# A transformer block on one core: the beginning reordered, and the q, k, v projection in five channel groups

## The chip, the core and the metric

One core of a Trainium2 chip runs the whole kernel as one program. The time is device microseconds of one execution; lower is better. TensorE multiplies matrices, VectorE (DVE) and ScalarE (ACT) work element by element, GpSimd (POOL) does almost nothing here, SyncE (SP) issues nearly all DMA transfers. Weights lie in HBM, working tiles in SBUF, and matmuls write to PSUM.

## The reference

One decoder layer on 256 tokens of width 2048, in float32:

```
mod = silu(c) @ w_ada + b_ada              # shift1, scale1, gate1, shift2, scale2, gate2
h   = rms_norm(x, norm1_gain) * (1 + scale1) + shift1
proj = h @ w_in                            # q, k, v of two attentions, q, k, v, r, a of a
                                           # gated linear attention, three branch gates
o_sb, o_dil, o_gla = the three token mixers on their columns
y   = g0 * (o_sb @ w_br_sb) + g1 * (o_dil @ w_br_dil) + g2 * (o_gla @ w_br_gla)
x   = x + gate1 * (y @ w_out)
h   = rms_norm(x, norm2_gain) * (1 + scale2) + shift2
x   = x + gate2 * ((silu(gate) * up) @ w_ffn_out)      # gate, up = split(h @ w_ffn_in)
```

All weights together are some 390 MB, and each is read once.

## The kernel before

**Matmuls in three parts.** Each float32 operand is split into a high part (`whi`, a cast to fp32r on ScalarE, line 142) and a low part (`wlo`, the difference, on VectorE, line 143). `mm3` (lines 147 to 150) multiplies high by high, high by low and low by high into one PSUM bank. `load_weights` (line 120) brings two chunks of 128 rows and 512 columns per DMA (512 KB) into `raw`, of which there are four buffers, as of `whi` and `wlo`. `block` (line 152) runs over the chunks of one block of 512 output columns and both tiles of 128 tokens. A block of all 16 chunks has 96 matmuls. There are four PSUM banks `acc` for these sums and four named `misc` for all else.

**The beginning** (lines 169 to 218, 324 to 351, 402 to 421). `crow`, `rows` and `brow` are small tiles into which c, the norm gains and the bias rows are loaded, to be transposed on TensorE into columns (`vec`, `bada`). They share the pool tag `scr` (three buffers) with the scratch tiles of all later work. `norm1` loads x in four pieces of 512 KB, squares it on ScalarE for the mean square (line 339), takes the inverse root per token tile (`rsqrt`, a chain of small operations on VectorE and ScalarE), scales x by it on ScalarE (line 346), transposes it in 32 transposes (line 350) and copies it from PSUM to `xT` (line 351).

**Shift and scale of norm 1** come from 2048 x 4096 of w_ada, for the channel chunks of one group at a time (`ada_group`, line 248). For each of 16 row chunks a tile with the shift and scale columns of the group is loaded (line 262) and multiplied by silu(c) and added on VectorE (`ada_mac`, lines 240 and 242). Then one column sum per chunk and segment on TensorE (`column_sum`, line 285) and small operations (lines 291 and 294) give two columns. `make_h` (line 355) applies them to `xT` and splits the result into the high and low h of that chunk (lines 360 to 362).

**Channel groups.** The 13 blocks of q, k, v columns are computed group by group over the 16 channel chunks, `GROUPS = ((0, 3), (3, 7), (7, 11), (11, 16))`, so that the first matmul needs shift and scale of three chunks only. While a group is multiplied, w_ada tiles of the next one are loaded and added, spread over the blocks (lines 423 to 433). After each group a block's sums leave PSUM: the first time as a ScalarE copy into an SBUF tile `A` (line 390), later as a VectorE addition onto it (line 392). The block with which a group ends is the one with which the next begins, and its sums stay in PSUM (`carried`): one block per boundary. The last group is mixed with the attentions (lines 699 to 705): blocks 0 to 4, stick-breaking attention, the gate columns of the linear attention (line 523, with its sum in an `acc` bank), blocks 9 to 12, the linear attention, blocks 5 to 8, the dilated attention. Behind them come the r and gate blocks, over all 16 chunks each.

**Order.** The program is written in order; a scheduler gives each engine a fixed order at build time, by priority. Loads and splits of weights, the w_ada work and the evacuations are given the priority of work 4000 instructions earlier (`prio`, line 97). `XAT = 4` says how many w_ada tiles of the first group are asked for before x. Each engine, SP among them, then goes through its own list in order, and one waiting instruction holds up what is behind it.

Of the kernel before, what the change touches and what calls it, by code (L numbers as in the profile page):

```python
# [17 lines left out]
P = 128  # L18
T = 256
# [14 lines left out]
XAT = 4  # L34
AHEAD = 4000
FIN = 13
GROUPS = ((0, 3), (3, 7), (7, 11), (11, 16))
# [27 lines left out]
def trunk(ctx: ExitStack, tc: tile.TileContext, I, out):  # L65
# [30 lines left out]
    @contextmanager  # L96
    def prio(offset=AHEAD):
        """Priority of work emitted ``offset`` instructions earlier; the count goes on."""
        with tc.high_priority(offset=offset):
            start = tc.cur_priority  # L100
            yield
            n = tc.cur_priority - start
        tc.cur_priority += n
# [15 lines left out]
    # ---------------------------------------------------------------- weights  # L119
    def load_weights(src, k0, k1, c0, w=NB, spare=()):  # L120
        """hi and lo parts of the 128-row chunks [k0, k1) of columns [c0, c0 + w).

        The last chunks go into the slots named in ``spare``, two slots for two chunks.
        """
# [27 lines left out]
    def block(pss, act, src, k0, k1, c0, base=0, w=None, tiles=range(NT), go_on=False, more=False):  # L152
        """pss[t] = act[:, chunks]^T @ src[chunks, c0:c0+512]; act(k, t) gives the hi and lo chunk."""
# [14 lines left out]
    # ---------------------------------------------------------------- constants  # L168
# [13 lines left out]
    crow = scr([P, P])  # L182
# [11 lines left out]
    rows = scr([P, P])  # L194
    brow = scr([P, P])
# [24 lines left out]
    def rsqrt(ss, inv_n, shape):  # L220
        """(ss * inv_n + EPS) ** -0.5, with a Newton step after the tables."""
# [12 lines left out]
    # ---------------------------------------------------------------- adaLN  # L234
# [13 lines left out]
    def ada_group(k0, k1, tags=ADA_TAGS, between=None):  # L248
        """shift and scale of norm 1 for the channel chunks [k0, k1): (scale + 1) * gain and shift as columns."""
# [37 lines left out]
    def finish_columns(ps, dst, seg, k0, gain_row=None):  # L287
        """adds the bias; with a gain, (scale + 1) * gain."""
# [9 lines left out]
    def ada_segment_steps(acc, seg):  # L298
        """multiply-adds of one segment; each runs well behind the load of its tile"""
# [21 lines left out]
    # ---------------------------------------------------------------- norm 1 and its transpose  # L321
    xT = [S(f"T{j}", [P, 4, T]) for j in range(4)]

    def norm1():
        xin = [S(f"A{9 + j}", [P, 2, NB]) for j in range(4)]
        for t in range(NT):
            for hf in range(2):
                nc.sync.dma_start(
                    xin[2 * t + hf].rearrange("p a b -> p (a b)"),
                    I["x"][t * P : (t + 1) * P, hf * 2 * NB : (hf + 1) * 2 * NB],  # L330
                )
        for t in range(NT):
            ss2 = small([P, 2])
            for hf in range(2):
                junk = scr([P, 512])
                xs = xin[2 * t + hf]
                pa = small([P, 2])
                for q in range(2):
                    nc.scalar.activation(junk, xs[:, q, :], AF.Square, accum_out=pa[:, q : q + 1])
                nc.vector.tensor_add(ss2[:, hf : hf + 1], pa[:, 0:1], pa[:, 1:2])  # L340
            ss = small([P, 1])
            nc.vector.tensor_add(ss, ss2[:, 0:1], ss2[:, 1:2])
            rstd = rsqrt(ss, 1.0 / D, [P, 1])
            for hf in range(2):
                xs = xin[2 * t + hf]
                nc.scalar.activation(xs, xs, AF.Copy, scale=rstd)
                for q in range(2):
                    ps = misc_bank([P, 4, P])
                    for i in range(4):
                        nc.tensor.transpose(ps[:, i, :], xs[:, q, i * P : (i + 1) * P], ident)  # L350
                    nc.scalar.copy(xT[2 * hf + q][:, :, t * P : (t + 1) * P], ps)
# [3 lines left out]
    def make_h(k, sh, sc):  # L355
        """hi and lo of x * sc + sh for channel chunk k."""
# [11 lines left out]
    # ---------------------------------------------------------------- input projection (q, k, v), by channel groups  # L368
    w_in = I["w_in"]
    A = [None] * 13  # L370
    # one group ends with the block that the next begins with: its sums stay in PSUM
    up, down = list(range(13)), list(range(12, -1, -1))
    orders = (up[1:] + up[:1], up, down)
    carried = []

    def proj_block(g, b, w=None, carry=False):
        k0, k1 = GROUPS[g]
        go_on = bool(carried)
        pss = carried.pop() if go_on else [acc_bank() for _ in range(NT)]
# [43 lines left out]
    for g in range(len(GROUPS) - 1):  # L423
# [3 lines left out]
        for n, b in enumerate(orders[g]):  # L427
            while done < steps * (n + 1) // FIN and next(nxt, "end") != "end":
                done += 1
            proj_block(g, b, early if (g, n) == (0, 0) else None, carry=n == 12)  # L430
# [5 lines left out]
    # small constants, needed from here on  # L436
# [19 lines left out]
    def qk_norm(b, h0, h1, gain):  # L456
        """rms norm of the heads h0..h1 of block b, transposed in place to [channel, token]; gain(h) is a column."""
# [21 lines left out]
    # ---------------------------------------------------------------- stick-breaking attention  # L479
# [41 lines left out]
    # ---------------------------------------------------------------- gated linear attention  # L521
    def gla():
        aw = load_weights(w_in, 0, KC, COL_A, P)
        ps = acc_bank([P, T])
# [27 lines left out]
        # q and k by channel: [channel, head, token], in place  # L552
# [80 lines left out]
    # ---------------------------------------------------------------- dilated attention  # L633
    def dilated():
# [25 lines left out]
        # mixture of the groups: softmax over their log-denominators  # L660
# [19 lines left out]
        for j in range(2):  # L680
            o = misc_bank([P, T])
            for g in range(3):
# [5 lines left out]
                # transposed as [s, t]: (s0, t0) | (s0, t1) | (s1, t1)  # L688
# [18 lines left out]
    # ada segments in the background: gate1 as rows, shift2 and scale2 as columns  # L707
# [45 lines left out]
    # ---------------------------------------------------------------- r, branch gates  # L753
# [29 lines left out]
    # GLA output: norm gain and silu(r), transposed  # L783
# [253 lines left out]
```

## Time and profile before

| | us |
|---|---|
| median of three runs (1648.91 to 1657.99) | 1654.28 |
| span of the profiled execution, first to last instruction | 1657.5 |
| highest of the three runs | 1657.99 |
| TensorE busy with matmuls | 1608.4 |
| VectorE busy | 1158.9 |
| ScalarE busy | 777.5 |

The times do not say which run the profile is of; its span lies 0.5 us under the highest. In the lines of the profile, "out<-in" names the tiles written and read, "xN" counts instructions, and what stands in brackets is the idle time of the engine ahead of the instruction and what ended it. A line of the timeline gives start, time to the last end, engine, line and operation. A line of the windows view gives a stretch, its length, the busy time and number of instructions of each engine (PE, PE's weight loads, DVE, ACT, POOL), the granted clock of TensorE, the DMA share and GB/s. PE stands for TensorE.

### The profile page before, as it was taken

What the parts mean: (1) busy time and instruction counts of PE and PEld (TensorE: products, weight loads), DVE (VectorE), ACT (ScalarE), POOL (GpSimd) and SP (SyncE); (2) the same over time, 40 slices, a digit from 0 to 9 for tenths busy, and PEclk for the clock granted to TensorE, in tenths of its full rate; (3) what the DMA queues carried; (4) which work ended last, traced back from release to release, by engine and by line L of the source; (5) the groups of instructions that cost most, each with busy time, mean ns of one, the idle gap of its engine ahead of it and who ended that gap; (6) DMA issues with size and microseconds to landing.
All of it is one profiled execution on the core that took longest, in us unless ns stands there. A gap on an engine that the chain in (4) does not pass through costs nothing.

```text
span 1657.5 us, 20010 instructions
## 1 busy us (share of the span) xinstructions
PE 1608.4 (97%) x7293; PEld 1323.2 (80%) x7293; DVE 1158.9 (70%) x1399; ACT 777.5 (47%) x1075; POOL 5.9 (0%) x14
## 2 busy tenths in 40 slices
PE   4999999999999999999999999999999999999998
PEld 3778888788888878788777788788888888888887
DVE  6789997888997577758876578765555555555554
ACT  5654446556765433343435643453344443344442
POOL 1000000000000000000000000000000000000000
PEclk9999999999999999999999999999999999999999
DMA  9999986445797789879987488955666665666664
GB/s 312 319 318 320 329 288 203 140 141 189 255 309 251 234 272 317 281 253 315 304 277 250 137 304 308 310 180 191 194 190 189 194 188 189 193 197 187 188 202 135
DMA packets 194563, 395.93 MB, mean 239 GB/s; under 512 B 12898, under 2 KB 27912, under 8 KB 194464
## 3 DMA queue, kind: packets, MB, share of 16 engines
q1 hardware_dynamic: 194240, 394.63, 73.5%
q8 instruction: 57, 0.93, 0.2%
q14 instruction: 42, 0.34, 0.1%
q0 software_dynamic: 224, 0.01, 0.0%
HBM read 392.50 MB, written 2.10 MB: 238 GB/s over the span
## 4 chain that ended last, share of the span: by engine, by line
PE 83%; DMA 7%; DVE 5%; ACT 2%; issue 2%; SPq 0%; DVEq 0%; ACTq 0%
PE acc L149 26%; PE acc L150 26%; PE acc L148 26%; DMA araw<-w_ada 4%; DVE wlo L143 2%; DVE ada L242 1%; ACT whi L142 1%; DMA raw<-w_ffn_in 1%; PE misc L582 1%; PE misc L834 1%; PE misc L285 1%; DMA raw<-w_in 1%; DVE T L242 1%; DMA A<-x 0%; PE misc L476 0%
## 5 line engine op out<-in xcount | busy, mean ns | idle before, releaser
L143 DVE TENSOR_TENSOR wlo<-raw,whi 128x1024 fp32r<-128x1024 f32 (+1 forms) x547 | 652.1, 1197 | 381.5 <-ACT whi L142 379.3
L142 ACT CAST whi<-raw 128x1024 fp32r<-128x1024 f32 (+1 forms) x547 | 563.1, 1032 | 732.5 <-PE acc L150 562.3
L149 PE MATMUL acc<-wlo,H 128*128 128x512 f32 x1552 | 607.8, 392 | 3.4 <-DVE wlo L143 3.2
L148 PE MATMUL acc<-whi,H 128*128 128x512 f32 x1552 | 606.3, 392 | 2.2 <-ACT whi L142 2.1
L150 PE MATMUL acc<-whi,H 128*128 128x512 f32 x1552 | 607.5, 392 | 0.0
L149 PEld LDWEIGHTS acc<-wlo,H 128*128 128x128 f32 x1552 | 292.0, 188 | 65.8 <-DVE wlo L143 6.3
L148 PEld LDWEIGHTS acc<-whi,H 128*128 128x128 f32 x1552 | 291.9, 188 | 64.1 <-ACT whi L142 3.9
L150 PEld LDWEIGHTS acc<-whi,H 128*128 128x128 f32 x1552 | 292.0, 188 | 61.0 <-DVE H L362 0.9
L148 PE MATMUL acc<-whi,A 128*128 128x512 f32 x360 | 141.7, 394 | 2.7 <-ACT whi L142 2.7
L149 PE MATMUL acc<-wlo,A 128*128 128x512 f32 x360 | 141.8, 394 | 0.5 <-DVE wlo L143 0.5
L150 PE MATMUL acc<-whi,A 128*128 128x512 f32 x328 | 128.9, 393 | 0.0
L242 DVE SCALAR_TENSOR_TENSOR T<-araw,csil,T 128x1024 f32<-128x1024 f32 x60 | 76.2, 1281 | 17.1 <-DMA araw<-w_ada 16.9
L242 DVE SCALAR_TENSOR_TENSOR ada<-araw,csil,ada 128x1024 f32<-128x1024 f32 x60 | 76.2, 1280 | 13.6 <-DMA araw<-w_ada 13.4
L148 PEld LDWEIGHTS acc<-whi,A 128*128 128x128 f32 x360 | 68.3, 190 | 17.4 <-ACT whi L142 3.1
L149 PEld LDWEIGHTS acc<-wlo,A 128*128 128x128 f32 x360 | 68.2, 190 | 15.6 <-DVE wlo L143 1.4
L150 PEld LDWEIGHTS acc<-whi,A 128*128 128x128 f32 x328 | 62.3, 190 | 12.8
L392 DVE TENSOR_TENSOR A<-A,acc 128x512 f32<-128x512 f32 x72 | 48.0, 684 | 10.1 <-PE acc L150 9.8
L150 PE MATMUL acc<-whi,T 128*128 128x512 f32 x120 | 47.3, 394 | 0.0
L148 PE MATMUL acc<-whi,T 128*128 128x512 f32 x120 | 47.3, 394 | 0.0
L149 PE MATMUL acc<-wlo,T 128*128 128x512 f32 x120 | 47.2, 393 | 0.0
L242 DVE SCALAR_TENSOR_TENSOR ada<-OS,csil,ada 128x1024 f32<-128x1024 f32 (+2 forms) x33 | 35.5, 1075 | 0.8 <-DMA OS<-w_ada 0.6
L148 PE MATMUL acc<-whi,OS 128*128 128x512 f32 x80 | 32.0, 399 | 0.0
(292 smaller groups left out, 1129.2 us busy)
## 6 DMA issues: line engine op xcount, KB each, us to landing
raw<-w_in SPq DMA_DIRECT2D x205, 512.0 KB, 4.7
raw<-w_ffn_in SPq DMA_DIRECT2D x176, 512.0 KB, 3.9
araw<-w_ada SPq DMA_DIRECT2D x128, 512.0 KB, 5.0
raw<-w_ffn_out SPq DMA_DIRECT2D x88, 512.0 KB, 4.5
raw<-w_out SPq DMA_DIRECT2D x32, 512.0 KB, 5.5
OS<-w_ada SPq DMA_DIRECT2D x16, 512.0 KB, 9.4
raw<-w_br_gla SPq DMA_DIRECT2D x16, 512.0 KB, 5.9
raw<-w_in SPq DMA_DIRECT2D x26, 256.0 KB, 4.9
```

The source lines that it names most:

```text
L142: nc.scalar.copy(hi[:, :n, :], raw[:, :n, :])
L143: state["split"] = nc.vector.tensor_tensor(lo[:, :n, :], raw[:, :n, :], hi[:, :n, :].bitcast(F32), op=ALU.subtract)
L148: nc.tensor.matmul(ps, lh, rh, start=start, stop=False)
L149: nc.tensor.matmul(ps, lh, rl, start=False, stop=False)
L150: state["mm"] = nc.tensor.matmul(ps, ll, rh, start=False, stop=stop)
L242: nc.vector.scalar_tensor_tensor(acc, raw, c, acc, op0=ALU.mult, op1=ALU.add)
L285: nc.tensor.matmul(ps, acc, ones[:, 0:1], start=True, stop=True)
L392: nc.vector.tensor_add(A[b][:, t, :], A[b][:, t, :], pss[t])
L582: nc.tensor.matmul(ps[:, h, :], at(lhs, h, t), at(rhs, h, t), start=True, stop=True)
L834: nc.tensor.transpose(ps[:, i, :], src[:, i * P : (i + 1) * P], ident)
```

## The change

- `crow`, `rows` and `brow` get slots of their own (`H7`, `H6`, `H5`, which later hold parts of h), in place of `scr`.
- `XAT` goes from 4 to 1: x is asked for behind one w_ada tile.
- `norm1` collects the squares of both token tiles ahead of one `rsqrt`; three pieces are squared on ScalarE, the fourth is squared and summed on VectorE. x is no longer scaled: a diagonal matrix of the inverse roots per token tile is made on VectorE, and a plain matmul of x with it both transposes and scales.
- Five groups in place of four, of 2, 3, 3, 4 and 4 chunks; at each boundary two blocks stay in PSUM, in a changed order of blocks. All other sums are added in SBUF as before.
- The gate columns of the linear attention sum in a `misc` bank in place of an `acc` bank.

Comments and docstrings also go, which does nothing to the program. The core of the diff:

```diff
-XAT = 4
+XAT = 1
-GROUPS = ((0, 3), (3, 7), (7, 11), (11, 16))
+GROUPS = ((0, 2), (2, 5), (5, 8), (8, 12), (12, 16))
...
-    crow = scr([P, P])
+    crow = S("H7", [P, P])
-    rows = scr([P, P])
-    brow = scr([P, P])
+    rows = S("H6", [P, P])
+    brow = S("H5", [P, P])
...
+        part = small([P, 2, NT])
         for t in range(NT):
-            ss2 = small([P, 2])
-            for hf in range(2):
-                junk = scr([P, 512])
-                xs = xin[2 * t + hf]
-                pa = small([P, 2])
-                for q in range(2):
-                    nc.scalar.activation(junk, xs[:, q, :], AF.Square, accum_out=pa[:, q : q + 1])
-                nc.vector.tensor_add(ss2[:, hf : hf + 1], pa[:, 0:1], pa[:, 1:2])
-            ss = small([P, 1])
-            nc.vector.tensor_add(ss, ss2[:, 0:1], ss2[:, 1:2])
-            rstd = rsqrt(ss, 1.0 / D, [P, 1])
             for hf in range(2):
                 xs = xin[2 * t + hf]
-                nc.scalar.activation(xs, xs, AF.Copy, scale=rstd)
-                for q in range(2):
-                    ps = misc_bank([P, 4, P])
-                    for i in range(4):
-                        nc.tensor.transpose(ps[:, i, :], xs[:, q, i * P : (i + 1) * P], ident)
-                    nc.scalar.copy(xT[2 * hf + q][:, :, t * P : (t + 1) * P], ps)
+                junk = S(f"H{t}", [P, 2, NB])
+                if (t, hf) == (NT - 1, 1):
+                    nc.vector.tensor_mul(junk, xs, xs)
+                    nc.vector.reduce_sum(part[:, hf, t : t + 1], junk.rearrange("p a b -> p (a b)"), axis=AX.X)
+                else:
+                    nc.scalar.activation(junk, xs, AF.Square, accum_out=part[:, hf, t : t + 1])
+        ss = small([P, NT])
+        nc.vector.tensor_add(ss, part[:, 0, :], part[:, 1, :])
+        rstd = rsqrt(ss, 1.0 / D, [P, NT])
+        diag = S("H3", [P, NT, P])
+        for t in range(NT):
+            nc.vector.tensor_scalar(diag[:, t, :], ident, rstd[:, t : t + 1], None, op0=ALU.mult)
+        for j in range(4):
+            for t in range(NT):
+                ps = misc_bank([P, 4, P])
+                for i in range(4):
+                    xs = xin[2 * t + j // 2][:, j % 2, i * P : (i + 1) * P]
+                    nc.tensor.matmul(ps[:, i, :], xs, diag[:, t, :], start=True, stop=True)
+                nc.scalar.copy(xT[j][:, :, t * P : (t + 1) * P], ps)
...
-    up, down = list(range(13)), list(range(12, -1, -1))
-    orders = (up[1:] + up[:1], up, down)
+    up = [1, 0] + list(range(2, 13))
+    down = [11, 12] + list(range(10, -1, -1))
+    orders = (up, down, up, down[:-2] + [0, 1])
...
-        go_on = bool(carried)
-        pss = carried.pop() if go_on else [acc_bank() for _ in range(NT)]
+        go_on = bool(carried) and not carry
+        pss = carried.pop(0) if go_on else [acc_bank() for _ in range(NT)]
...
-            proj_block(g, b, early if (g, n) == (0, 0) else None, carry=n == 12)
+            proj_block(g, b, early if (g, n) == (0, 0) else None, carry=n >= 11)
...
         aw = load_weights(w_in, 0, KC, COL_A, P)
-        ps = acc_bank([P, T])
+        ps = misc_bank([P, T])
```

## The prediction

> **What bounds the kernel now.** I read the page first.
>
> ```profile
> span 1657.5 us, 20010 instructions
> PE 1608.4 (97%) x7293; PEld 1323.2 (80%) x7293; DVE 1158.9 (70%) x1399; ACT 777.5 (47%) x1075; POOL 5.9 (0%) x14
> PE 83%; DMA 7%; DVE 5%; ACT 2%; issue 2%; SPq 0%; DVEq 0%; ACTq 0%
> ```
>
> TensorE carries 83% of the chain that ended last. The change leaves its projection matmuls as many as they are, so it can only move what stands between them: the time before the first one, and the stalls. A busy PE says little about stalls; the spacing of starts does. The timeline of PE in an undisturbed place:
>
> ```profile
> 63.80 0.39 PE L148 MATMUL acc<-whi,H 128*128 128x512 f32 x1
> ...
> 65.84 0.39 PE L148 MATMUL acc<-whi,H 128*128 128x512 f32 x1
> ```
>
> Nine matmuls in 2.04 us: **0.2267 us each**. With it I price each channel group of q, k, v. A group of c chunks is 13 blocks x 2 token tiles x 3 x c matmuls: 234 for three chunks, 312 for four. The windows of the matmuls on `acc`, cut at the first matmul of each group, show these counts (a window counts one on its edge twice):
>
> ```profile
> 35.12:96.17 61.05, 56.84 (x234) 0.97 0.91 312
> 96.17:169.24 73.07, 71.30 (x313) 1.00 0.94 323
> 169.24:242.66 73.42, 71.67 (x313) 1.00 0.94 310
> ```
>
> The columns are stretch, length, PE busy, clock, DMA share, GB/s. 234 x 0.2267 = 53.05 and 312 x 0.2267 = 70.73, so the groups lose 8.0, 2.3 and 2.7 us. With 35.13 us before the first matmul, **48.1 us** stand beside matmuls up to the last group. The same windows for all engines (DVE is the third pair):
>
> ```profile
> 0.00:10.00 10.00, 0.26 (x1) 0.18 (x1) 3.42 (x7) 1.76 (x3) 0.69 (x6) 1.00 0.78 242
> 10.00:20.00 10.00, 3.11 (x15) 3.11 (x16) 5.68 (x14) 8.11 (x21) 3.57 (x7) 1.00 0.90 330
> 20.00:30.00 10.00, 4.72 (x21) 3.75 (x19) 8.50 (x17) 6.94 (x15) 0.00 (x0) 1.00 0.96 324
> ...
> 169.24:242.66 73.42, 73.42 (x333) 60.71 (x332) 71.23 (x100) 30.92 (x35) 0.00 (x0) 1.00 0.94 310
> ...
> 340.00:392.00 52.00, 51.88 (x293) 44.07 (x292) 50.21 (x70) 25.47 (x35) 0.00 (x0) 1.00 0.50 147
> ```
>
> Two things bind. Until 30 us it is DMA (shares 0.90 and 0.96). From the third group on VectorE is full: 71.23 of 73.42 us, 97%, and 50.21 of 52 inside the attention stage, while PE still loses almost nothing. The timeline of the start:
>
> ```profile
> 3.18 2.12 SPq L328 DMA_DIRECT2D A<-x  x4
> 11.00 0.63 ACT L339 ACTIVATE scr<-A 128x512 f32<-128x512 f32 x1 [7.93 <-DMA A<-x]
> 13.86 0.33 SPq L200 DMA_DIRECT2D scr<-norm_gain  x1
> 16.89 3.67 PE L350 MATMUL misc<-ident,A 128*128 128x128 f32 x16 [14.04 <-ACT A L346]
> 18.52 0.33 SPq L201 DMA_DIRECT2D scr<-b_ada  x1
> 22.45 0.46 SPq L262 DMA_DIRECT2D A<-w_ada  x1
> 30.48 1.02 DVE L242 SCALAR_TENSOR_TENSOR ada<-A,csil,ada 128x768 f32<-128x768 f32 x1
> 31.64 2.33 PE L285 MATMUL misc<-ones,ada 128*128 128x1 f32 x12 [2.62 <-DVE ada L242]
> 35.13 1.22 PE L148 MATMUL acc<-whi,H 128*128 128x512 f32 x2 [1.16 <-ACT whi L142]
> 36.39 1.22 PE L149 MATMUL acc<-wlo,H 128*128 128x512 f32 x2
> 37.41 1.14 PE L150 MATMUL acc<-whi,H 128*128 128x512 f32 x2
> 38.35 0.63 PE L148 MATMUL acc<-whi,H 128*128 128x512 f32 x1
> 38.78 0.44 PE L149 MATMUL acc<-wlo,H 128*128 128x512 f32 x1
> 39.05 0.39 PE L150 MATMUL acc<-whi,H 128*128 128x512 f32 x1
> ```
>
> The sixteenth w_ada tile is issued at 22.45 and its multiply-add starts at 30.48. Column sums, h and the first weight cast follow; the first matmul comes 3.5 us after the first sum.
>
> **The change, part by part.**
>
> *First group of two chunks.* The start loads 4 x 512 KB of x and 16 w_ada tiles, of 384 KB before and 256 KB after: 8.39 and 6.29 MB. The 2.10 MB saved are 6.4 us at 324 to 330 GB/s, so the last tile comes at about 30.4 - 6.4 = 24.0 us. The last multiply-add shrinks from 0.94 to 0.67 us, and the sums from 12 records to 8, of 2.33 / 12 = 0.19 us.
>
> *Own rooms.* SP stood behind row loads that waited for `scr`: the rows at 13.86 and 18.52, with seven w_ada tiles behind. The DMA share of 0.90 against 0.96 bounds what that cost at 0.7 us; the transfers already issued covered the rest. I take 0.3. The seven POOL loads are off the path.
>
> *x second.* Its four issues pass three w_ada tiles on SP, each 2.12 / 4 = 0.53 us. The same bytes must land before the first matmul, so this gains nothing by itself. It brings all of x by about 11 us (2.36 MB: 9.8 us at 242 GB/s, and a landing).
>
> *Statistics.* VectorE takes one square and its reduction (two passes of 1024, some 2.3 us by the 1.22 us of a split below), one rsqrt chain and two diagonals. I put the diagonals at 15.9 us.
>
> *rstd in the transposing matmul.* The rows of the three kinds:
>
> ```profile
> L350 PE MATMUL misc<-ident,A x32: 421/421/475, 16.9 to 28.1; 128*128 128x128 f32 x32
> L560 PE MATMUL misc<-ident,A x16: 272/273/327, 334.8 to 336.5; 128*128 128x128 f32 x16
> L495 PE MATMUL misc<-A,A x12: 379/380/484, 280.3 to 323.8; 128*128 128x256 f32 x12
> ```
>
> A transpose leaves one record (L350: 8 chunks x 2 halves x 2 tiles = 32). A plain f32 matmul leaves two: line 495 runs once for each of six heads, and there are 12. So 32 transposes become 64 passes. A pass takes 3.67 / 16 = 0.229 us early on and (336.5 - 334.8) / 15 = 0.113 late. Bounds: 7.2 to 14.7 us. The first eight projection matmuls need 3.9 us (35.13 to 39.05) before the spacing falls to 0.2267, so I take 17 slow passes and 47 fast ones: 9.2 us, ending at 25.1, just behind the multiply-adds. That makes the first matmul **28.5** (25.1 and 3.4 behind it: the first h waits for the first sums alone, so fewer sums save little there). Bounds: 27.0, by DMA alone (24.0 + 0.7 + 3.0, less 0.7 of SP), and 33.9, with all passes slow (15.9 + 14.7 + 3.3).
>
> [...]
>
> *Group 0.* 156 matmuls, 35.4 us. Of the 8.0 lost, the slow start is 2.1 (3.92 us for eight matmuls), the sums of group 1 (16 records of 0.11) 1.8, and waits for weights 4.1. The DMA need is 12.6 MB, 38 us at 330 GB/s, against 35.4, with about 2 MB loaded ahead. So its waits stay about as they are. I take 6.0: half the slow start, as TensorE works from 16 to 25 us and idles for three before the first matmul, 1.3 for 12 records of sums, 3.7 of waits. Bounds: 4.4 (no slow start, 3.1 of waits) and 8.
>
> *Five groups, two carried.* The numbers of weight tiles (9 per block) and w_ada tiles (80, the same widths) are unchanged. Evacuations by addition go from 72 to 88: 65 - 8 = 57 per token tile, less 13 first copies, twice. What one costs, from VectorE's timeline and groups:
>
> ```profile
> 186.38 1.28 DVE L392 TENSOR_TENSOR A<-A,acc 128x512 f32<-128x512 f32 x2
> 187.58 1.22 DVE L143 TENSOR_TENSOR wlo<-raw,whi 128x1024 fp32r<-128x1024 f32 x1
> 188.71 1.53 DVE L242 SCALAR_TENSOR_TENSOR ada<-T,csil,ada 128x512 f32<-128x512 f32 x2
> ```
>
> ```profile
> 42.69 0.69 DVE L143 TENSOR_TENSOR wlo<-raw,whi 128x512 fp32r<-128x512 f32 x1 [0.55 <-ACT whi L142]
> ```
>
> ```profile
> L242 DVE SCALAR_TENSOR_TENSOR T<-araw,csil,T 128x1024 f32<-128x1024 f32 x60 | 76.2, 1281 | 17.1 <-DMA araw<-w_ada 16.9
> ```
>
> Start to start an addition is 0.60, a split 1.13, so 0.08 of each duration overlaps: half a split 0.61, a multiply-add of 1024 columns 1.20, of 768 0.94, of 512 0.67. The 16 additions are 9.6 us of VectorE. Test on the group 169 to 243: 26 x 1.13 + 15 x 0.67 + 15 x 0.94 + 24 x 0.60, with an estimated 3.5 of small work and h, is 71.4 of 73.4, as shown. After the change:
> - group 1 (3 chunks, next 3): VectorE 50 against 55.4 of PE. Lost: 2.3.
> - group 2 (3, next 4): 13 x 1.74 + 18.7 + 22 x 0.60 + 2.2 = 56.7, at 97.5% filled 58.0, against 53.05 for PE. **Lost: 5.0**, between 2.5 (the four weight buffers absorb it) and 6. DMA is near its limit as well: 18.6 MB in 58 us, 321 GB/s.
> - group 3 (4, next 4): 64 against 73.3. Lost: 2.7.
>
> The four carried PSUM banks at a boundary delay nothing that could run: no block of the next group starts without its h.
>
> *Last group.* Four chunks in place of five: 78 matmuls or 17.7 us less, which stand earlier instead. The gate matmul in `misc` keeps its passes; I cost it at nothing, since four misc banks were never the late side there (bound 2 us).
>
> **Sum.** 28.5 + 6.0 + 2.3 + 5.0 + 2.7 = 44.5 against 48.1: 3.6 us less. The profiled span 1657.5 becomes 1653.9. That span is 3.2 above the median of the runs shown (1654.28); on the median it is **1650.7**.
>
> **Rivals.**
> 1. *All covers hold.* First matmul at 27.0, an open clock (4.4 lost in group 0), the weight buffers absorb group 2 (2.5): 27.0 + 4.4 + 2.3 + 2.5 + 2.7 = 38.9, or 9.2 less: **1645.1**. For it: the group before with VectorE at 97% lost only 2.7. Against: group 2 asks for 6% more than VectorE has.
> 2. *Slow passes.* PE ends x's transposes at 30.6, first matmul 33.9: **1656.1**, no change. For it: all 32 transposes before ran at 0.229.
> 3. *Attention has its own chain (slower).* If the last group's stretch is set by attention on VectorE and not by PE, the 17.7 us taken out of it come back as idle PE: up to **1668.4**. It decides once the r and gate blocks can't be drawn forward to fill; it is over 0.5% slower if 12 of the 17.7 come back. For it: VectorE 50.21 of 52. Against: PE is full there too (51.88), so fillers exist.
> 4. *The 16 additions are paid in full*, 9.6 in place of the 2.3 in group 2: 1658.0, no change.
>
> **Chances and range.** 0.5% is 8.3 us, about what a measurement of this kernel can tell from no change. Forecast 0.42, rival 1 0.30, rival 2 0.09, rival 3 0.14, rival 4 0.05. Faster 0.30, within 0.56, slower 0.14. The range goes from 1641 (rival 1, with the 4 us by which runs stray from their median) to 1664 (rival 3 at three quarters).
>
> **What would show it.** First projection matmul at 27 to 30 us; 64 records of the transposing matmul, most at 0.113; group 0 in 41 us, group 2 near 58 with VectorE at 97%; last group's start near 256.6 (242.66 + 17.7 - 3.6); no new PE gaps in attention. A first matmul after 32, or gaps over 1 us between 257 and 400, make the forecast wrong, and then rivals 2 or 3 hold. So does a shift in the later stages, which I take as unchanged.

## The result, and the profile after

The changed kernel takes **1669.47 us** (median of 7 runs, 1664.18 to 1674.34) beside 1657.99 us for the kernel before in the same series (7 runs, 1648.91 to 1662.54): a ratio of **1.0083, 95% interval 1.0065 to 1.0101**. It is slower, by some 0.8%, where 0.2% faster (1650.7 beside 1654.28) was the forecast.

The head of the page of the changed kernel: span and instructions, busy time by engine, and further down the shares of the chain that ended last.

```profile
span 1667.7 us, 20056 instructions
...
PE 1612.5 (97%) x7325; PEld 1328.2 (80%) x7325; DVE 1164.1 (70%) x1409; ACT 773.5 (46%) x1061; POOL 5.8 (0%) x14
...
PE 77%; DMA 11%; DVE 7%; issue 3%; ACT 2%; SPq 0%; DVEq 0%; ACTq 0%
```

The span is 10.2 us longer, PE is busy for 4.1 us more, so some 6 us are new idle time of PE. PE's share of the chain falls from 83 to 77%; DMA and VectorE have what it lost. Lines of code stand one to seven higher than before (`make_h` is now 366 to 368, the weighted additions of w_ada 241 and 243, the column sums 286, the transposing matmul 356, the evacuating addition 399).

The windows of the matmuls on `acc`, cut at the first matmul of each group (length, PE busy and count, clock, DMA share, GB/s):

```profile
36.38:76.10 39.72, 38.61 (x156) 0.92 0.85 285
76.10:130.54 54.44, 53.34 (x235) 1.00 0.97 325
130.54:187.56 57.02, 53.82 (x235) 1.00 0.94 320
187.56:270.29 82.73, 76.20 (x313) 0.94 0.86 288
270.29:371.00 100.71, 74.99 (x313) 1.00 0.47 147
```

With 0.2267 us for each of 156, 234, 234 and 312 matmuls the groups lose 4.3, 1.4, 4.0 and **12.0** us. The first projection matmul comes at **36.39**. That makes 58.1 beside matmuls, where before had 48.1 and the forecast 44.5. The start of the changed kernel:

```profile
1.25 0.63 POOL L210 DMA_DIRECT2D H<-sb_q_gain  x1 [0.81 <-POOLq L1029]
...
4.82 0.22 POOL masks.py:197 MEMSET ident<- 128x128 f32 x1
...
13.37 1.54 DVE L243 SCALAR_TENSOR_TENSOR ada<-A,csil,ada 128x512 f32<-128x512 f32 x2 [6.19 <-DMA A<-w_ada]
...
14.83 1.22 DVE L340 TENSOR_TENSOR H<-A 128x1024 f32<-128x1024 f32 x1
...
15.97 0.74 DVE L243 SCALAR_TENSOR_TENSOR ada<-A,csil,ada 128x512 f32<-128x512 f32 x1
16.63 1.21 DVE L341 TENSOR_REDUCE tiny<-H 128x1 f32<-128x1024 f32 x1
...
18.42 0.15 DVE L345 TENSOR_TENSOR tiny<-tiny 128x2 f32<-128x2 f32 x1
...
18.54 0.75 DVE L243 SCALAR_TENSOR_TENSOR ada<-A,csil,ada 128x512 f32<-128x512 f32 x1
19.20 0.16 DVE L224 TENSOR_SCALAR tiny<-tiny 128x2 f32<-128x2 f32 x1
...
23.14 0.48 DVE L350 TENSOR_SCALAR H<-ident,tiny 128x128 f32<-128x128 f32 x2
...
23.48 9.90 PE L356 MATMUL misc<-H,A 128*128 128x128 f32 x64 [17.74 <-DVE H L350]
...
33.66 0.53 PE L286 MATMUL misc<-ones,ada 128*128 128x1 f32 x4
...
36.39 0.80 PE L148 MATMUL acc<-whi,H 128*128 128x512 f32 x1 [1.19 <-ACT H L366]
```

The root's chain is made of operations of 0.15 to 0.20 us, yet it takes from 18.42 to 23.14: behind each of them VectorE does a multiply-add of w_ada (0.75 us) before it comes to the next. From the moment VectorE starts again (13.37) to the diagonals it does ten of them, some 7 us.

One table of where the time stands, in profiled time. "Moved by" compares the n-th matmul of lines 148 to 150, counted from the first, with the same matmul of the kernel before; the 900th lies in q, k, v ahead of the attentions, the 2100th behind the three attentions.

| us | forecast | after | before |
|---|---|---|---|
| first projection matmul | 28.5 | 36.4 | 35.1 |
| lost in the groups ahead of the last | 6.0, 2.3, 5.0, 2.7 | 4.3, 1.4, 4.0, 12.0 | 8.0, 2.3, 2.7 |
| sum | 44.5 | 58.1 | 48.1 |
| moved by, 900th matmul | -3.6 | +10.0 | |
| from the 900th to the 2100th | 0 | +2.8 | |
| from the 2100th to the last | 0 | -3.0 | |

**The stall of group 3.** The timeline of the changed kernel from the column sums of group 3's channels over the boundary at 187.57:

```profile
183.01 1.84 PE L286 MATMUL misc<-ones,ada 128*128 128x1 f32 x16
...
185.82 2.35 DVE L143 TENSOR_TENSOR wlo<-raw,whi 128x1024 fp32r<-128x1024 f32 x2
...
187.57 0.62 PE L148 MATMUL acc<-whi,H 128*128 128x512 f32 x2
...
188.09 1.28 DVE L243 SCALAR_TENSOR_TENSOR ada<-T,csil,ada 128x1024 f32<-128x1024 f32 x1
...
189.30 1.22 DVE L143 TENSOR_TENSOR wlo<-raw,whi 128x1024 fp32r<-128x1024 f32 x1
...
190.74 1.23 DVE L143 TENSOR_TENSOR wlo<-raw,whi 128x1024 fp32r<-128x1024 f32 x1 [0.22 <-ACT whi L142]
191.88 1.28 DVE L243 SCALAR_TENSOR_TENSOR ada<-OS,csil,ada 128x1024 f32<-128x1024 f32 x1
...
193.08 1.57 DVE L368 TENSOR_TENSOR H<-scr,H 128x256 fp32r<-128x256 f32 x4
...
193.55 1.22 PE L150 MATMUL acc<-whi,H 128*128 128x512 f32 x2 [2.24 <-DVE H L368]
...
193.59 0.60 ACT L367 ACTIVATE scr<-T,mod 128x256 f32<-128x256 f32 x1 [2.38 <-DVE H L368]
...
194.57 0.63 PE L148 MATMUL acc<-whi,H 128*128 128x512 f32 x1
```

And what PE waited for there, in us, times and longest; the row with the sums belongs to the second stall, at 243:

```profile
PE acc L150 <- DVE H L368: 2.2, 1, 2.2
PE misc L286 <- DVE ada L243: 1.3, 1, 1.3
PE acc L148 <- ACT whi L142: 0.7, 1, 0.7
PE acc L149 <- DVE wlo L143: 0.5, 1, 0.5
```

The sums are over at 184.9. ScalarE has the first row that VectorE needs for a low part of the next h (line 367) at 186.86, and the third at 189.78; a low part (line 368) is 0.4 us of VectorE. But on VectorE the low parts stand behind four splits and two multiply-adds, the next group's weights and w_ada tiles, until 193.08. PE gets as far as it can with high parts, waits three times (for a cast, for a split, and longest for the low part of h; its starts are 1.07, 0.92 and 2.63 us apart), and then runs its next matmuls 0.427 us apart, at a granted clock of 0.50, until 199.3. Up to there 7.0 of the 12.0 us are gone. The rest is 1.8 us for 16 sums of the last group, a wait of 1.4 for them at 243, and some 1.6 behind it at a clock of 0.50 (247.2 to 250.6).

### The profile page after: what moved, and what is told of

Same layout as the page of the kernel before. It is cut to its first block, busy times and chain, and to the rows that moved or that the text cites. A ratio compares the mean times of both kernels' runs of the same rounds, so it can differ in the third digit from the quotient of the medians.

```text
span 1667.7 us, 20056 instructions
## 1 busy us (share of the span) xinstructions
PE 1612.5 (97%) x7325; PEld 1328.2 (80%) x7325; DVE 1164.1 (70%) x1409; ACT 773.5 (46%) x1061; POOL 5.8 (0%) x14
## 4 chain that ended last, share of the span: by engine, by line
PE 77%; DMA 11%; DVE 7%; issue 3%; ACT 2%; SPq 0%; DVEq 0%; ACTq 0%
PE acc L150 24%; PE acc L149 23%; PE acc L148 23%; DMA araw<-w_ada 6%; DVE wlo L143 2%; DVE T L243 1%; ACT whi L142 1%; DMA raw<-w_ffn_in 1%; DVE ada L243 1%; DMA raw<-w_in 1%; PE misc L589 1%; PE misc L286 1%; PE misc L841 1%; DMA raw<-w_br_gla 1%; DMA raw<-w_br_sb 1%
## 5 line engine op out<-in xcount | busy, mean ns | idle before, releaser
L399 DVE TENSOR_TENSOR A<-A,acc 128x512 f32<-128x512 f32 x88 | 58.1, 682 | 6.0 <-PE acc L150 5.3
L243 DVE SCALAR_TENSOR_TENSOR ada<-OS,csil,ada 128x768 f32<-128x768 f32 (+2 forms) x35 | 38.9, 1111 | 1.8 <-DMA OS<-w_ada 1.6
```

What stands on the lines that cost most here:

```text
L243: nc.vector.scalar_tensor_tensor(acc, raw, c, acc, op0=ALU.mult, op1=ALU.add)
L399: nc.vector.tensor_add(A[b][:, t, :], A[b][:, t, :], pss[t])
```

## The experiments

The theory after this result: the five groups cost, not the beginning, and they cost at the boundary into group 3, by VectorE's order, with the half clock behind it. Rivals: VectorE's load (16 additions more), the second carried block, the shorter last group, the bank of the gate columns. Each ratio below is to the kernel before on the same chip, with its 95% interval; where none stands, the kernel was timed once.

### The two halves of the change

`d1_new_beginning`: before, with the new beginning only.

```diff
-XAT = 4
+XAT = 1
 GROUPS = ((0, 3), (3, 7), (7, 11), (11, 16))
...
-    crow = scr([P, P])
+    crow = S("H7", [P, P])
...
-            rstd = rsqrt(ss, 1.0 / D, [P, 1])
...
+        rstd = rsqrt(ss, 1.0 / D, [P, NT])
...
+                    nc.tensor.matmul(ps[:, i, :], xs, diag[:, t, :], start=True, stop=True)
```

> The kernel before with the new beginning alone (own rooms, x second, one root, diagonal matmul), four groups and one carried block as before. Theory: the new beginning does not bring the first matmul forward, because the chain of the statistics ends late on VectorE and 64 passes stand behind it; with 384 KB tiles the w_ada side (30 us) and the passes end together, so the first projection matmul comes at 36 to 38 us and the time is 0 to 3 us over the kernel before. Rival (the beginning is fine and the loss lies in the groups): first matmul at 33 to 35 us, time 0 to 2 us under before. Either way the 10 us of the change must not appear here.

`d2_new_groups`: the changed kernel with the old beginning (the reverse of the diff above, with the five groups).

> The changed kernel with the old beginning (rows in scr, x fifth, scaled x and 32 transposes), and the five groups with two carried blocks. Theory: with the smaller first group and the old statistics the first projection matmul comes at 30 to 31 us, 5 us before the kernel before; the boundaries in front of groups 3 and 4 still lose some 9 us as in the changed kernel, so the time is 2 to 6 us over before. Rival (the beginning carries the loss): under before by 4 us or more.

Measured: d1 **0.9991 (0.9979 to 1.0003)**, 1654.78 us; d2 **1.0109 (1.0089 to 1.0130)**, 1674.04 us. The loss belongs to the groups. The new beginning alone is at most a little faster; its first matmul stands at 36.00, no earlier than before's 35.13. With the old beginning and two-chunk first group the first matmul stands at 31.73, ahead of the changed kernel's 36.39: the shorter group does start earlier, and the reordered beginning starts later.

### The boundary

`d3_h_first`: the next group's rows are made with raised priority, ahead of splits and multiply-adds.

```diff
         for _ in nxt:
             pass
-        h_group(g + 1)
+        with prio():
+            h_group(g + 1)
```

> The changed kernel with one edit: h of the next group gets the priority of the weight splits. Theory: at the boundary at 188 us TensorE waits for low parts of h that stand on VectorE behind splits and multiply-adds; with h ahead of them the waits of 2.6 and 1 us and the slow clock behind them go: 6 to 8 us under the changed kernel. Rival (VectorE has too little time in all, through the 16 additions): the wait moves to the splits, at most 2 us under the changed kernel.

Measured: 1664.03 us, **1.0042 (1.0026 to 1.0057)**. VectorE and PE at the same boundary in d3:

```profile
182.09 1.84 PE L286 MATMUL misc<-ones,ada 128*128 128x1 f32 x16
...
184.91 1.22 DVE L143 TENSOR_TENSOR wlo<-raw,whi 128x1024 fp32r<-128x1024 f32 x1
...
186.04 0.76 DVE L368 TENSOR_TENSOR H<-scr,H 128x256 fp32r<-128x256 f32 x2
...
186.65 0.62 PE L148 MATMUL acc<-whi,H 128*128 128x512 f32 x2
186.71 1.22 DVE L143 TENSOR_TENSOR wlo<-raw,whi 128x1024 fp32r<-128x1024 f32 x1
...
187.11 0.39 PE L149 MATMUL acc<-wlo,H 128*128 128x512 f32 x1
...
187.85 0.76 DVE L368 TENSOR_TENSOR H<-scr,H 128x256 fp32r<-128x256 f32 x2
```

Two low parts now come behind one split, the other two behind a second. The line moves ScalarE's rows of h as well: its four pairs run from 183.46 to 187.51 in one go, where in the changed kernel they begin at 185.76, with casts between them. Group 3 loses 2.0 us in place of 12.0, and the 900th matmul stands 1.0 us ahead of before's in place of 10.0 behind. Half of the loss in timed runs is gone with one line; at the last matmul 5.4 us stay in this profile (9.8 in the changed kernel's), all lost behind the projection groups.

`f1_fewer_adds`: the changed kernel, 16 additions fewer in group 2 (the sums that they would add are left out).

```diff
-                else:
+                elif g != 2 or b < 3:
                     nc.vector.tensor_add(A[b][:, t, :], A[b][:, t, :], pss[t])
```

> The changed kernel without the additions of eight blocks in the third group (16 additions, 9.6 us of VectorE; the sums of these chunks are left out). Theory of load: VectorE then has 10 us of room before the boundary at 188 us, the last multiply-adds, column sums and h come earlier, the waits of 1.1, 0.9 and 2.6 us there go, 7 to 10 us under the changed kernel. Rival (order alone: low parts of h behind splits, however much room there is): the waits at the boundary stay, at most 3 us under the changed kernel.

Measured: 1659.09 us, **0.9994 (0.9970 to 1.0019)**. The length of group 2 stays (it loses 4.2, as against 4.0), but the sums for group 3 come at 175.0 in place of 183.0, and group 3 loses 1.9. So the load decides how late the sums come, and the order decides what that costs: either one mended removes the stall. It is no rule without exception. In s1 below, which has h first too, the profiled execution (1669.8 us, where the median is 1660.11) still loses 6.2 us in group 3, with a wait of 1.2 us for the last multiply-add ahead of the sums, the second stall of the changed kernel.

What holds group 2 is less clear. ScalarE's longest waits from 130 to 187.5 in the changed kernel, in us, times and longest:

```profile
ACT whi L142 <- DMA raw<-w_in: 21.6, 12, 4.0
```

and in the third group of the kernel before, 169 to 243:

```profile
ACT whi L142 <- DMA raw<-w_in: 4.9, 2, 2.9
```

The casts wait for weights to land, at a DMA share of 0.94. But SP issued those loads late, waiting for VectorE to split an earlier tile and so free its buffer:

```profile
SPq L131 <- DVE wlo L143: 37.5, 22, 3.7
```

The 4.0 us of group 2 are the 16 sums and one wait for a cast (starts 2.04 us apart at 167.7). In f1 that wait is gone, ScalarE's waits for weights are 10.0 us in place of 21.6, and a shorter wait ahead of the sums (0.45 us), with matmuls 0.427 apart behind them (177.7 to 180.7), takes its place. Loads and VectorE's splits wait for each other here, and no run separates them.

`h2_last_four`: before, with groups of 3, 4, 5 and 4 chunks.

```diff
-GROUPS = ((0, 3), (3, 7), (7, 11), (11, 16))
+GROUPS = ((0, 3), (3, 7), (7, 12), (12, 16))
```

> The kernel before with groups of 3, 4, 5 and 4 chunks: a last group of four chunks in place of five, no other part of the change, as many additions as before, and VectorE not overfilled in any group (68 of 71 and 75 of 88 us). Theory that attention loses cover when 17.7 us of matmuls are taken out of its group: the last group starts 17.7 us later, and 2 to 5 us of that are still missing at 600 us. Rival (fillers take the place of the cover): within 1 us of before at 600 us and at the end.

Measured: 1672.04 us, **1.0085 (1.0057 to 1.0113)**. The attentions lose 0.5 us from the 900th to the 2100th matmul, so a shorter last group is not what costs there. Group 1 of h2 loses 6.5 us, where before loses 2.3, with two waits for splits of 1.5 each, and group 2 (five chunks) loses 9.7. A stall of the other kind, the second one of the changed kernel, has part in that loss: PE's waits in h2 from 225 to 245 hold one row.

```profile
PE misc L285 <- DVE ada L242: 2.9, 1, 2.9
```

PE came to the sums before the last multiply-add and stood idle for 2.93 us ahead of 233.60.

### The carried blocks and the bank

`d5_two_carried`: before with two carried blocks, and the gate columns in a `misc` bank.

```diff
-    up, down = list(range(13)), list(range(12, -1, -1))
-    orders = (up[1:] + up[:1], up, down)
+    up = [1, 0] + list(range(2, 13))
+    down = [11, 12] + list(range(10, -1, -1))
+    orders = (down, up, down[:-2] + [0, 1])
...
-        ps = acc_bank([P, T])
+        ps = misc_bank([P, T])
```

> The kernel before with two carried blocks in its four groups (66 additions in place of 72, the gate columns of the linear attention in a misc bank), and nothing else of the change. Theory: carrying is harmless; the loss comes from the small groups. 0 to 4 us under before. Rival (four PSUM banks held over a boundary stall TensorE there): a gap of over 1 us at 96, 169 or 243 us, and 3 to 9 us over before.

`x2_h_first_one_carried`: d3 with one block carried (and eight additions more).

> The changed kernel with h first and one carried block per boundary in place of two (96 additions in place of 88). Theory that two carried blocks, whose four banks and changed order reach into the last group, delay attention: from the start of the last group to the matmul number 2100 it loses 4.3 us against before with two; with one it loses under 1, and the time is 1 to 4 us under h first. Rival (the shorter last group gives less cover): the 4 us stay, and the 8 more additions add 0 to 3 us.

Measured: d5 1658.71 us, **1.0014 (0.9994 to 1.0034)**, with no new wait at its boundaries (its group 0 loses 9.4, where before loses 8.0); x2 1664.64 us, **1.0057 (1.0039 to 1.0075)**. The second carried block is not the cause. In x2 the attentions lose 4.7 us as in d3 (4.4), so that loss does not come from carrying either.

`m2_misc_alone`: before with the gate columns in a `misc` bank (the diff). `m3_h_first_acc`: d3 with the same line the other way round, back to `acc`.

```diff
         aw = load_weights(w_in, 0, KC, COL_A, P)
-        ps = acc_bank([P, T])
+        ps = misc_bank([P, T])
```

> The kernel before with one edit of the change: the sum of the gate columns of the linear attention in a misc bank. Theory: this, and not the shorter last group or the carried blocks, is what attention loses: its 48 matmuls no longer run beside the first head of the stick-breaking attention, so TensorE idles there or a later stage comes later; nothing changes up to 279 us, and at matmul number 2100 it is 2 to 5 us behind before. Rival (the bank is of no weight): within 1 us there.

> The changed kernel with h first and the gate columns in an acc bank as before. Theory of the bank: the 4.3 us that h first alone loses from the start of the last group (number 900) to number 2100 shrink to under 1, and the time is 3 to 5 us under h first alone, a ratio of 1.001 to 1.0025 to before. Rival (shorter last group): no change, 1.003 to 1.006.

`m4_acc_alone_undone`: the line undone in the changed kernel, and nothing else.

> The changed kernel with one edit: the gate columns' chain takes its bank from the projection's ring again, as before the change. If the bank has a cost of its own in this kernel (on top of the reordered boundary taking it back brought 1664.03 - 1658.17 = 5.9 us), this reads about 1663.5, a ratio of 1.004 to the kernel before. If the bank costs only where the boundary's stall is gone, or not at all (alone on the kernel before it read 0.9999), this stays at 1669 to 1670, 1.008.

Measured: m2 1656.91 us, **0.9999 (0.9982 to 1.0017)**; m3 1658.17 us, **0.9999 (0.9985 to 1.0014)**, against d3's 1.0042; m4 1668.36 us, **1.0059 (1.0038 to 1.0080)**, against 1.0083, intervals that overlap. The two lines of m3 together, h first and the bank, take back the whole loss of the changed kernel. The attentions, from the 900th to the 2100th matmul, moved by, in single profiles:

| | gate columns in `acc` | in `misc` | difference |
|---|---|---|---|
| before's groups | 0 (before) | +2.8 (m2) | 2.8 |
| five groups | +1.6 (m4) | +2.8 (after) | 1.2 |
| five groups, h first | +2.5 (m3) | +4.4 (d3) | 1.9 |

So the bank costs 1 to 3 us in the attentions in each pair, and the five groups 1.6 to 2.5 us more that no edit here explains. Each figure is of one execution, but the other profiles fall in the same order: before's groups with `acc` moved by -0.8 to 0.5 (d1, b2, h2), with `misc` by 3.4 (d5); five groups with `acc` by 1.4 and 2.1 (s1, n1), with `misc` by 2.4 to 5.2 (d2, d4, e1, f1, g1, k1, x2). PE's waits with the bank alone (m2), 363 to 584, against 1.9 us in all in before:

```profile
PE misc L476 <- DVE A L469: 2.3, 2, 1.3
PE misc L691 <- DVE T L687: 1.7, 1, 1.7
PE misc L623 <- ACT scr L626: 0.5, 1, 0.5
```

They sum to 4.5, but m3, with the old bank, has 3.8 at the same lines: the waits tell of order, not of the bank itself. In before's groups the later stages give the time back (m2 stands 0.4 us ahead at the last matmul). Whether a loss in the attentions lasts depends on what stands behind it; that part is not settled.

### The beginning

`e1_chain_first`: norm 1 with a higher priority than the w_ada work.

```diff
-        with prio():
+        with prio(20000):
             norm1()
+        with prio():
             load_vectors()
```

> The changed kernel with the statistics of x at a higher priority than the w_ada multiply-adds. Theory: the diagonals come at 16 to 19 us in place of 23.1, the 64 passes end at 26 to 29, and the first projection matmul comes at 30 to 32 in place of 36.4: 4 to 6 us under the changed kernel. Rival (the multiply-adds pushed back, or the loads, then set the start): first matmul at 35 or later, within 1 us.

`s1_chain_on_gpsimd`: m3 with the small operations of the root on GpSimd, out of VectorE's list.

```diff
-        rstd = rsqrt(ss, 1.0 / D, [P, NT])
+        nc.gpsimd.tensor_scalar(v, ss, 1.0 / D, EPS, op0=ALU.mult, op1=ALU.add)
+        nc.scalar.activation(rstd, v, AF.Ln)
+        nc.scalar.activation(rstd, rstd, AF.Exp, scale=-0.5)
+        nc.gpsimd.tensor_mul(z, rstd, rstd)
...
```

> The kernel of the run before this one with the small operations of the root chain on GpSimd in place of VectorE, where a w_ada multiply-add stood between each two of them. Theory: the diagonals come at 20 to 21 us in place of 23.1, the 64 passes end at 30, first projection matmul at 33 to 34.5 in place of 36.5, the boundary into the fourth group 1 to 3 us earlier. Rival (the chain is slow by its hops between engines, not by what stands between): the diagonals at 22.5 us or later.

`g1_no_statistics`: the changed kernel with ones for the inverse roots, so without the norm. `k1_h_first_no_statistics`: the same in d3.

```diff
-        rstd = rsqrt(ss, 1.0 / D, [P, NT])
+        rstd = ones[:, 0:NT]
```

> The changed kernel with ones in place of the inverse roots: the squares and sums are made but nothing waits for the root chain (the norm is left out). Theory: the diagonals come before x, the 64 passes start with x at 12 to 13 us and end by 23, and the first projection matmul comes at 30 to 31 us, behind the w_ada multiply-adds, in place of 36.4. Rival (w_ada and the weights set the start anyway): 34 us or later.

> The changed kernel with h ahead of the splits and, in addition, ones in place of the inverse roots (the norm is left out), so that the first projection matmul comes at 30.6 us in place of 36.7. Theory that loads set the boundary into the fourth group: 12.9 MB must still come for groups 1 and 2 at a rate near its limit, so the boundary stays at 186 to 188 us as with h first alone (186.7), group 2 loses 3 to 6 us more, and the time is within 2 us of h first alone (ratio 1.0042 to before, so 1.003 to 1.006). Rival (an earlier start is worth what it is): boundary at 181 to 182 us, 5 to 6 us under h first alone, a ratio of 1.0005 to 1.002.

`d4_transposes`: x scaled on ScalarE and transposed in 32 transposes, the rest of the beginning as changed.

```diff
-            nc.vector.tensor_scalar(diag[:, t, :], ident, rstd[:, t : t + 1], None, op0=ALU.mult)
+                nc.scalar.activation(xs, xs, AF.Copy, scale=rstd[:, t : t + 1])
...
-                    nc.tensor.matmul(ps[:, i, :], xs, diag[:, t, :], start=True, stop=True)
+                    nc.tensor.transpose(ps[:, i, :], xs, ident)
```

> The changed kernel with x scaled on ScalarE and transposed with the identity as before, all else of the beginning as changed. Theory that the root chain sets the start, and not the passes: the diagonals are gone, four scalings of 1.1 us stand in their place, 32 passes in place of 64, and the first projection matmul comes at 33.5 to 36, at most 3 us before 36.4. Rival (the 64 passes set it): 31 or earlier.

`n1_old_beginning_h_first_acc`: m3 with the old beginning.

> Five groups with two blocks carried, the next group's rows first at the boundaries, the gate columns in the projection's ring, and the beginning as it was before the change. With the new beginning this arrangement read 0.9999. If the new beginning is worth what it brought in four groups (0.9991 against 1, 1.5 us) up to what it brought in five unmended ones (1674.04 - 1669.47 = 4.6 us), this reads 1.001 to 1.003, some 1659.5 to 1663. If group 2, which waits for its weights, swallows the earlier start, this reads 1.000, 1658.

| | ratio (interval), or us | diagonals | first projection matmul |
|---|---|---|---|
| after | 1.0083 (1.0065 to 1.0101) | 23.14 | 36.39 |
| e1 chain first | 1.0086 (1.0065 to 1.0106) | 21.58 | 35.23 |
| s1 chain on GpSimd | 1.0017 (0.9998 to 1.0037); m3 0.9999 | 21.3 | 34.49 |
| g1 no statistics | 1670.08 us | | 30.57 |
| k1 the same, h first | 1.0028 (1.0011 to 1.0046); d3 1.0042 | | 30.22 |
| d4 transposes | 1673.72 us | | 33.93 |
| m3, for s1 and n1 | 0.9999 (0.9985 to 1.0014) | | 35.72 |
| n1 old beginning | 1.0022 (1.0004 to 1.0039); m3 0.9999 | | 32.58 |

A higher priority alone did little: in e1 the multiply-adds still stand between the root's operations. It seems that the list gives the place of an operation that waits for a result to one that is ready; that was only argued. On GpSimd, out of VectorE's way, the diagonals come at 21.3, and the first matmul 1.2 us ahead of m3's (s1). With transposes in place of the 64 passes (32 records, 6.71 us) the first matmul comes 2.5 us sooner (d4). Without the root the first matmul comes 5.8 us sooner (g1), so the root's chain is the largest part of what the start waits for. But a sooner start is not always a sooner end: g1 reaches group 3 at the same 187.6 as the changed kernel, since it then loses 8.9 us in group 2, with waits for a cast and for h. With h first some of it lasts: k1 starts 6.5 us ahead of d3, loses 6.3 in group 0 where d3 loses 2.9, and reaches group 3 at 183.27, 3.4 ahead of d3's 186.65. That lies between its theory (186 to 188) and its rival (181 to 182). By its ratio it is some 2 us ahead of d3, with intervals that overlap. The old beginning, whose first matmul is 3.1 us ahead of m3's, is no faster (1.0022 against 0.9999). In all three pairs (d1 and before, the changed kernel and d2, m3 and n1) the new beginning reads 0.1 to 0.3% lower; by each pair alone the intervals overlap.

### A mended version

`b2_beginning_h_first`: d1 with d3's line; before's four groups.

> Version to keep: the kernel before (four groups, one carried block) with the new beginning and h first. The new beginning alone was 0.9991 of before. Theory: h first is worth little where the boundaries don't stall, 0 to 2 us; ratio 0.997 to 0.9995. Rival (other order of VectorE costs elsewhere): 1.000 or more.

Measured: 1659.05 us, **1.0014 (0.9999 to 1.0030)**, where 0.997 to 0.9995 was hoped for. No version beats the kernel before by more than its interval: d1 (0.9991) and m3 (0.9999) are level with it.

## Why the prediction was wrong, step by step

- **The statistics, "I put the diagonals at 15.9 us": the first failing step.** They came at 23.14, 7.2 us late, and the first matmul at 36.39 in place of 28.5. What follows the diagonals was forecast as 12.6 us and took 13.2. The chain was priced by its own operations, as if VectorE had nothing else; its list holds ten multiply-adds of w_ada between 13.37 and 23.14. Of the 7.2 us, x's last piece has 1.3 (it landed at 12.33, not 11), the wait of VectorE's list for w_ada and two multiply-adds ahead of the square 2.5, and the eight multiply-adds that stand between the square, the reduction and the root's operations the remaining 3.4. g1 shows what the root costs the start (30.57 without it).
- **The transposing matmul: right.** 64 records, 9.90 us against 9.2, with 24 slow passes (starts 0.21 us apart) in place of 17 and 40 at 0.11. Rival 2 gave 33.9 for slow passes throughout; 40 were not slow, so the late start is not that rival's.
- **Own rooms, "off the path": not quite.** The seven row loads no longer wait, so POOL issues them first and begins the identity at 4.82. c's transpose needs it and moves from 2.59 to 5.46. The transfers cover this: the second w_ada tile's multiply-add waited for DMA until 13.37.
- **Group 0, group 1, group 2: right in size, in part by luck.** 4.3, 1.4 and 4.0 against 6.0, 2.3 and 5.0. Group 0 was made up otherwise: its 14 matmuls up to 42.5, at a clock of 0.50, cost 2.9 where 1.0 was put for the slow start, the sums 1.3 as forecast, and the 3.7 of waits for weights did not come. That half of the slow start would stay was the author's estimate, and no run shows it: m3's first six matmuls start within 1.26 us, 0.1 over five times 0.2267. Group 1 lost its sums alone. In group 2 the reason was not settled: VectorE is at 96% (55.02 of 57.02 us), but taking 16 additions away left its loss at 4.2, in another place. The loads (DMA share 0.94, 320 GB/s), which the prediction named as near their limit and did not charge, have a part in it.
- **"Group 3: lost 2.7": the failing step that makes it slower.** 12.0. VectorE's load was compared with PE's over a whole group, which says nothing of a boundary: there four operations of 0.4 us stood behind some 7 us of work for later. Before, the sums for the boundary at 169 ran twelve us ahead, two of the four low parts were made ahead of it, behind splits and multiply-adds as well, and that order cost nothing:

```profile
156.68 1.93 PE L285 MATMUL misc<-ones,ada 128*128 128x1 f32 x16
...
161.59 0.42 DVE L362 TENSOR_TENSOR H<-scr,H 128x256 fp32r<-128x256 f32 x1
...
168.21 0.42 DVE L362 TENSOR_TENSOR H<-scr,H 128x256 fp32r<-128x256 f32 x1
```

After, the sums ran 4.6 us ahead and no low part. Putting h first (d3) or taking load away (f1) brings the loss to 2.0 and 1.9.
- **The attention "at nothing (bound 2 us)": wrong.** +2.8 from the 900th to the 2100th matmul in the profile. The bank has 1.2 to 2.8 of it in three pairs, the five groups the rest. In timed runs it weighs nothing alone (m2, 0.9999) and 0.4% once h is first (d3 1.0042, m3 0.9999), and why is not shown. h2 speaks against rival 3's mechanism (a shorter last group): 0.5. That the time came out on rival 3's side, slower, is luck.
- **Rival 4, the additions paid in full:** by the time alone it fits (f1 is 10.4 us faster than the changed kernel), by the place it does not: the group that has the additions is no shorter without them, and d3 removes the same stall with all of them kept.
- **The later stages, "unchanged": -3.0 in this profile.** In the other profiles they moved by -7.1 (d5) to +4.3 (s1). The cause is left open.
- **The clock.** That the clock would be open at the first projection matmul was an estimate of rival 1. In the changed kernel it did not come: the passes start 0.21 us apart up to 28.5 and 0.11 from 28.8 (the clock reads 1.00 over both), and the clock reads 0.50 from 35.6 for 6.8 us, though group 0 lost less than forecast. In m3 it came: the clock reads 1.00 from 34 to 38, and the matmuls from 36.05 on start 0.23 us apart. In the kernel before, behind 2.6 us of idle PE, the clock reads 0.50 from 32.0 to 38.9: the first column sums start 0.11 us apart, those from 32.1 on 0.21.

The sum in the prediction's own form: of the 13.6 us between 44.5 and 58.1, the start has +7.9, group 3 +9.3, the other groups -3.6.

## What to carry to other kernels

A loaded engine must be read at the boundary, not by its share of the group: ask which of its operations the next stage waits for, and what stands ahead of them in its list. A short chain of small operations on a busy engine costs what stands between them, here 4.7 us for eight operations that sum to 1.3. And an earlier start can be lost in the stages behind it: all of 5.8 us in g1, about half of 6.5 us in k1.

## What the runs showed of the hardware

Short waits are paid twice here: with PE waits of 0.7, 0.5 and 2.2 us within 6 us the granted clock was 0.50 for 6.8 us (192.6 to 199.4), behind one wait of 1.3 us and 16 sums (243.1 to 246.6) for 3.4 us (247.2 to 250.6). Matmuls then start 0.427 apart in place of 0.2267. These stretches are 3.4 us or twice that. Not every wait brings one. The windows of the changed kernel and of m3 around the first projection matmul (PE, PEld, DVE, ACT, POOL, clock, DMA share, GB/s):

```profile
34.00:36.00 2.00, 0.79 (x6) 0.62 (x5) 1.91 (x7) 1.05 (x5) 0.00 (x0) 0.89 1.06 380
36.00:38.00 2.00, 1.61 (x4) 1.33 (x5) 2.00 (x6) 2.00 (x5) 0.00 (x0) 0.50 0.68 197
```

```profile
34.00:36.00 2.00, 0.81 (x5) 0.73 (x6) 2.00 (x10) 1.05 (x3) 0.00 (x0) 1.00 1.06 375
36.00:38.00 2.00, 2.00 (x10) 1.62 (x10) 2.00 (x4) 2.00 (x4) 0.00 (x0) 1.00 0.88 296
```

From 34 to 36 us PE is as idle in the one as in the other, and its idle stretch ahead of the first projection matmul is 1.19 us in both (35.20 to 36.39, 34.53 to 35.72); the clock falls in the first and stays in the second. Why one pattern has two outcomes is not shown.
